# A hybrid decoder trunk on one core: part of the second MLP product by seven block products instead of eight

## The chip, the core and the metric

The kernel runs on one core of one Trainium2 chip. The time is device microseconds of one execution. TensorE (PE) multiplies, VectorE (DVE) and ScalarE (ACT) do everything elementwise, GpSimd (POOL) only builds two small tables at the start, and SyncE (SP) issues the loads of the weights.

## What is computed

Two decoder layers over 256 tokens of width 2048, all in float32. The mixer of a layer (latent attention and retention) is not touched by the change; what follows it is:

```python
h = rmsnorm(x, mlp_norm[l])
x = x + jnp.square(jax.nn.relu(h @ w_up[l])) @ w_down[l]     # w_up 2048 x 8192, w_down 8192 x 2048
...
return rmsnorm(x, final_norm)
```

## The kernel before

**Numbers in two parts.** Each float32 value that PE multiplies is split into a high part, rounded to the multiplier's format, and a low part, the rest. A product is hi·hi + hi·lo + lo·hi. Activations lie with features on partitions and the 256 tokens along the free axis. In `mac_feat` a 128x128 piece of the weight's high part stays in PE while the activation's high and low parts stream past as 512 columns (L213); then the weight's low part, with the high 256 columns (L214). That is one pair of matmuls, 512 and 256 columns. ACT copies the second half of a PSUM bank out and DVE adds the first half (`join`, L231 and L232).

**The weights' way.** SP loads 512 KB of a weight into one of five `raw` buffers. ACT writes the high part into one of six `w` buffers (L179) and DVE the low part (L180, raw minus high). Such a tile of 128x1024 values feeds eight pairs of matmuls. `proj_feat` takes `nt` column tiles of 128 at once, one PSUM bank each, and goes over all k.

**The MLP** of a layer runs in two blocks of FB = 4096 hidden features. For each block, `w_up` in groups of four column tiles (eight w tiles a group, then four joins, relu², and the split of the result into `u` tiles), then `w_down` in groups of 4, 4, 4, 2, 2 column tiles over the block's 32 `u` tiles; each column tile is joined, multiplied by a row of norm factors (L674) and added to x (L675). In a layer's last block the new x is also scaled and split for the next layer (`xs`, L175/L176) and its squares are summed (L256/L257).

**Order.** The program is written in this order, and a scheduler lays out each engine's instructions ahead of time; each engine then goes through its own list in order, waiting on semaphores. At a group's end the four banks are complete; while DVE joins them, PE goes on with w tiles that were split earlier.

Of the kernel before, what the change touches and what calls it, by code (L numbers as in the profile page):

```python
# [11 lines left out]
F32 = mybir.dt.float32  # L12
# [6 lines left out]
P = 128  # L19
# [13 lines left out]

UP_TILES = 4
OUT_GROUPS = [(0, 4), (4, 4), (8, 4), (12, 2), (14, 2)]
END_GROUPS = [(0, 4), (4, 4), (8, 4), (12, 2), (14, 1), (15, 1)]
N_RAW, N_SPLIT = 5, 6

LONGER_ONES, LONGER_XS, LONGER_ROOT = 8, 24, 23

ROUND = 1.5 * 2.0 ** 23

# [43 lines left out]
def kernel(ctx: ExitStack, tc: tile.TileContext, xt, positions, w_in, w_uq, w_ukv, w_o, w_up, w_down,  # L88
# [20 lines left out]
    def w_tile(shape):  # L109
        return wpool.tile(shape, F32R, tag="w", name="w", bufs=N_SPLIT)  # L110

    def w_load(src, shape):
        raw = wpool.tile(shape, F32, tag="raw", name="raw", bufs=N_RAW)
# [23 lines left out]
    def gcol(i):  # L137
        return gain[:, i:i + 1]
# [173 lines left out]

    def norm_tiles():
        acc = cpool.tile([P, T], F32, tag="ssq", name="ssq")
        return acc, []

    def norm_step(acc, tiles, j, g0):
# [5 lines left out]
        tiles.append(xs)  # L323
        if acc is not None:
            add_square(acc, x[j], j == 0)

    acc, xs = norm_tiles()
    for j in range(KD):
        norm_step(None, xs, j, G_ATTN)

    def first_squares():
        for j in range(KD):
# [4 lines left out]
    for l in range(DEPTH):  # L337
        g0 = l * G_LAYER

        with tc.tile_pool(name=f"mix{l}", bufs=1) as ap:  # L340
# [290 lines left out]
            for c0, nt in OUT_GROUPS:  # L631
                for n, ps in enumerate(proj_feat(w_o[l], 0, c0 * P, mixed, nt)):
                    j = c0 + n
                    t = tmp()
                    join(ps, t)
                    nc.vector.tensor_tensor(x[j], x[j], t, op=ALU.add)
                    norm_step(acc, ms, j, g0 + G_MLP)


        with tc.tile_pool(name=f"mlp{l}", bufs=1) as up:  # L640
            rows = {}

            def square_rows(acc=acc):
                yield
                r2 = norm_col([acc], D)
                r22 = col("r22")
                nc.vector.tensor_tensor(r22, r2, r2, op=ALU.mult)
                yield
                yield
# [4 lines left out]
            acc_n, xs_n = norm_tiles() if not last_layer else (cpool.tile([P, T], F32, tag="ssq", name="ssq"), None)  # L654
            for b in range(FF // FB):
                us = []
                for c in range(0, FB, UP_TILES * P):
                    for ps in proj_feat(w_up[l], 0, b * FB + c, ms, UP_TILES):
                        t = tmp()
# [5 lines left out]
                end = last_layer and b == FF // FB - 1  # L665
                if end:
                    root = spool.tile([P, 1 + LONGER_ROOT], F32, tag="root", name="root", bufs=1)[:, 0:1]
                    nc.scalar.sqrt(root, ones)
                for c0, nt in END_GROUPS if end else OUT_GROUPS:
                    for n, ps in enumerate(proj_feat(w_down[l], b * FB, c0 * P, us, nt)):  # L670
                        j = c0 + n
                        t = tmp()
                        join(ps, t)
                        nc.vector.tensor_tensor(t, t, rows["rs2b"], op=ALU.mult)  # L674
                        nc.vector.tensor_tensor(x[j], x[j], t, op=ALU.add)  # L675
                        if end:
                            if j < KD - 1:
                                add_square(acc_n, x[j], j == 0)
                            else:
                                last_sq = tmp("sq", 2)  # L680
                                nc.scalar.activation(last_sq, x[j], AF.Square)
                            nc.scalar.activation(x[j], x[j], AF.Copy, scale=gcol(G_FINAL + j))
                        elif b == FF // FB - 1:
                            norm_step(acc_n, xs_n, j, (l + 1) * G_LAYER + G_ATTN)
            acc, xs = acc_n, xs_n


# [7 lines left out]

    keep_warm(8)
    v = col("nv")
    mean_squares(v, [acc, last_sq], D, EPS)
# [37 lines left out]
```

## Time and profile before

| what | value |
|---|---|
| median of three runs | 2185.0 us (2184.48 to 2185.58) |
| the profiled execution | 2185.49 us, its span 2183.7 us |
| TensorE's mean granted clock | 0.997 |
| busy: PE, PEld (weight loads), DVE, ACT | 99%, 87%, 66%, 49% of the span |
| DMA | 400 MB, mean 183 GB/s |

A busy share is the part of the span in which an engine had an instruction running; the chain of the page follows the work that ended last back to its start, and a wait is time in which an engine stood still, put down to whatever came last.

### The profile page before, as it was taken

How to read it: one execution, taken by the hardware profiler on the slowest of the kernel's cores; microseconds unless marked ns; L12 is line 12 of the kernel's file. 1: busy time of each engine (PE TensorE's matmuls, PEld its weight loads, DVE VectorE, ACT ScalarE, POOL GpSimd, SP SyncE). 2: the span in 40 equal slices, each digit the busy share in tenths (PEclk: the TensorE clock that was granted, in tenths of full speed). 3: DMA queues.
4: the chain of work that ended last, by engine and by line, in shares of the span. 5: the costliest groups of instructions: out<-in, count | busy, mean ns of one | idle time of the engine just before them, and what ended most of it. 6: DMA issues, size and time to landing. Idle time of an engine off the chain costs nothing.

```text
span 2183.7 us, 32563 instructions
## 1 busy us (share of the span) xinstructions
PE 2162.2 (99%) x12566; PEld 1907.8 (87%) x12566; DVE 1433.5 (66%) x2487; ACT 1077.9 (49%) x1658; POOL 24.2 (1%) x34
## 2 busy tenths in 40 slices
PE   7999999999999999999999999999999999999998
PEld 6888888888888888888898888888888888888887
DVE  8878976656555556655668888666665555655554
ACT  7555555545443444444455554555454344544453
POOL 4000000000000000000000000000000000000000
PEclk9999999999999999999999999999999999999999
DMA  7555556666556666555655555566665566665553
GB/s 245 170 160 179 151 188 192 183 194 184 197 180 200 184 194 192 188 190 192 189 173 151 174 164 173 174 198 188 192 189 189 193 187 191 185 196 189 192 183 97
DMA packets 273115, 400.07 MB, mean 183 GB/s; under 512 B 12608, under 2 KB 143808, under 8 KB 272960
## 3 DMA queue, kind: packets, MB, share of 16 engines
q1 hardware_dynamic: 272000, 397.08, 58.7%
q8 instruction: 98, 1.61, 0.3%
q10 hardware_dynamic: 960, 0.92, 0.1%
q14 instruction: 57, 0.47, 0.1%
HBM read 395.85 MB, written 2.10 MB: 182 GB/s over the span
## 4 chain that ended last, share of the span: by engine, by line
PE 98%; DVE 1%; ACT 0%; issue 0%; DMA 0%; SPq 0%; DVEq 0%
PE mm L213 57%; PE mm L214 29%; PE mm L218 3%; PE mm L219 1%; PE at L213 1%; PE at L214 1%; PE at L483 0%; PE at L484 0%; PE mm L368 0%; PE mm L367 0%; PE mm L369 0%; PE at L218 0%; PE at L516 0%; PE at L545 0%; DVE xs L176 0%
## 5 line engine op out<-in xcount | busy, mean ns | idle before, releaser
L180 DVE TENSOR_TENSOR w<-raw,w 128x1024 fp32r<-128x1024 f32 (+3 forms) x792 | 921.9, 1170 | 673.9 <-ACT w L179 673.0
L179 ACT CAST w<-raw 128x1024 fp32r<-128x1024 f32 (+3 forms) x792 | 795.3, 1008 | 887.6 <-PE mm L214 828.3
L213 PE MATMUL mm<-xs,w 128*128 128x512 f32 x2944 | 1032.6, 394 | 8.6 <-ACT w L179 8.6
L214 PE MATMUL mm<-xs,w 128*128 128x256 f32 x2944 | 824.2, 280 | 2.6 <-DVE w L180 2.4
L213 PE MATMUL mm<-u,w 128*128 128x512 f32 x2048 | 710.2, 392 | 0.0
L213 PEld LDWEIGHTS mm<-xs,w 128*128 128x128 f32 x2944 | 553.8, 188 | 129.4 <-ACT w L179 8.9
L214 PE MATMUL mm<-u,w 128*128 128x256 f32 x2048 | 572.4, 280 | 0.0
L214 PEld LDWEIGHTS mm<-xs,w 128*128 128x128 f32 x2944 | 553.9, 188 | 5.1 <-DVE w L180 4.8
L213 PEld LDWEIGHTS mm<-u,w 128*128 128x128 f32 x2048 | 384.4, 188 | 85.1
L214 PEld LDWEIGHTS mm<-u,w 128*128 128x128 f32 x2048 | 384.3, 188 | 0.0
L213 PE MATMUL mm<-mix,w 128*128 128x512 f32 x512 | 177.8, 392 | 0.0
L231 ACT COPY tb<-mm 128x256 f32<-128x256 f32 x280 | 99.6, 372 | 88.5 <-PE mm L214 84.5
L214 PE MATMUL mm<-mix,w 128*128 128x256 f32 x512 | 143.1, 280 | 0.0
L232 DVE TENSOR_TENSOR t<-mm,tb 128x256 f32<-128x256 f32 x280 | 108.2, 418 | 30.7 <-ACT tb L231 30.2
L213 PEld LDWEIGHTS mm<-mix,w 128*128 128x128 f32 x512 | 96.1, 188 | 21.1
L214 PEld LDWEIGHTS mm<-mix,w 128*128 128x128 f32 x512 | 96.1, 188 | 0.0
L218 PE MATMUL mm<-w,xs 128*128 128x512 f32 x256 | 93.0, 401 | 0.0
L219 PE MATMUL mm<-w,xs 128*128 128x256 f32 x256 | 71.7, 280 | 0.0
L172 ACT CAST u<-t 128x256 fp32r<-128x256 f32 x128 | 48.6, 405 | 27.4 <-DVE t L661 27.4
L218 PEld LDWEIGHTS mm<-w,xs 128*128 128x128 f32 x256 | 48.1, 188 | 10.7
L173 DVE TENSOR_TENSOR u<-t,u 128x256 fp32r<-128x256 f32 x128 | 48.9, 422 | 2.8
L219 PEld LDWEIGHTS mm<-w,xs 128*128 128x128 f32 x256 | 48.2, 188 | 0.0
(176 smaller groups left out, 1107.0 us busy)
## 6 DMA issues: line engine op xcount, KB each, us to landing
raw<-w_up SPq DMA_DIRECT2D x256, 512.0 KB, 4.4
raw<-w_down SPq DMA_DIRECT2D x256, 512.0 KB, 3.9
raw<-w_in SPq DMA_DIRECT2D x144, 512.0 KB, 4.6
raw<-w_o SPq DMA_DIRECT2D x64, 512.0 KB, 4.3
raw<-w_uq SPq DMA_DIRECT2D x16, 384.0 KB, 4.2
raw<-w_in SPq DMA_DIRECT2D x16, 320.0 KB, 3.1
raw<-w_ukv SPq DMA_DIRECT2D x8, 512.0 KB, 4.1
x<-xt SPq DMA_DIRECT2D x8, 256.0 KB, 6.7
```

What stands on the lines that cost most here:

```text
L172: nc.scalar.copy(head, src)
L173: nc.vector.tensor_tensor(dst[:, 1, :], src, head.bitcast(F32), op=ALU.subtract)
L179: nc.scalar.copy(dst_h, src)
L180: nc.vector.tensor_tensor(dst_l, src, dst_h.bitcast(F32), op=ALU.subtract)
L213: nc.tensor.matmul(ps, wk[:, 0, n0:n0 + P], act.rearrange("p s t -> p (s t)"), start=first, stop=False)
L214: nc.tensor.matmul(ps[:, 0:T], wk[:, 1, n0:n0 + P], act[:, 0, :], start=False, stop=last)
L218: nc.tensor.matmul(ps, act[:, 0, t0:t0 + P], wk, start=first, stop=False)
L219: nc.tensor.matmul(ps[:, 0:256], act[:, 1, t0:t0 + P], wk[:, 0], start=False, stop=last)
L231: nc.scalar.copy(tb, ps[:, T:2 * T])
L232: nc.vector.tensor_tensor(dst, ps[:, 0:T], tb, op=ALU.add)
```

## The change

Of the 2048 columns of `w_down`, the first 768 (six of the sixteen column tiles) are no longer done tile by tile. For each pair of hidden-feature tiles (u tiles 2k and 2k+1) the tokens are cut into two halves of 128, the hidden features into the two tiles, and the 768 columns into two halves of 384. The product of these 2x2 blocks is made from seven block products (Winograd's form of Strassen's scheme): four sums of `u` blocks (`first_factors`) and four of weight blocks (`second_factors`) are factors beside the plain blocks, and seven PSUM banks collect the products over the block's eight pairs. Here the `u` block stays in PE and 384 weight columns stream past, three matmuls to a product, 21 for a pair. The other ten column tiles are done singly (`next_tile`, in the eighth bank), one after each pair and two at the end; a layer's last block has none after pairs 3 and 7 and four at the end. FB falls from 4096 to 2048, so a layer has four blocks of 16 `u` tiles and not two of 32. At a block's end the seven banks are added to seven sums in SBUF (`gather_products`), at a layer's end the sums are combined, turned by 24 transposes in both layers together, and added to x. The norm factors are multiplied onto `u` (L760) instead of onto the outputs. In the changed file the lines of the helpers lie ten further down: L179/L180 is L189/L190, L213/L214 is L223/L224, L232 is L242, L173 is L183.

```diff
-FB = 4096
+FB = 2048
...
+SB = 384
+SN = 2 * SB // P
+TILE_AFTER, LAST_TILE_AFTER = range(8), (0, 1, 2, 4, 5, 6)
...
+MOVING = 16
...
-    def tmp(tag="t", bufs=4):
+    def tmp(tag="t", bufs=6):
...
+            def first_factors(k, t0, t1):
+
+                f = up.tile([P, 2, 4, P], F32R, tag=f"f{k}", name=f"f{k}")
+                sa, sb = tmp("t"), tmp("t")
+                nc.vector.tensor_tensor(sa[:, 0:P], t0[:, P:T], t1[:, P:T], op=ALU.subtract)
+                nc.vector.tensor_tensor(sa[:, P:T], t0[:, 0:P], t0[:, P:T], op=ALU.subtract)
+                nc.vector.tensor_tensor(sb[:, 0:P], sa[:, 0:P], t0[:, 0:P], op=ALU.subtract)
+                nc.vector.scalar_tensor_tensor(sb[:, P:T], sb[:, 0:P], -1.0, t1[:, 0:P], op0=ALU.mult, op1=ALU.subtract)
+                for i, q in enumerate((sa, sb)):
+                    split(f[:, :, 2 * i:2 * i + 2, :], q.rearrange("p (i t) -> p i t", i=2))
+                return f
+
+            def second_factors(r0):
+
+                raws = [w_load(w_down[l][r0 + k * P:r0 + (k + 1) * P, 0:2 * SB], [P, 1, 2 * SB])[:, 0, :] for k in range(2)]
+                w11, w12, w21, w22 = (r[:, n * SB:(n + 1) * SB] for r in raws for n in range(2))
...
+                parts([w11], w11)
+                parts([w21, w22], raws[1])
+                sums = [wpool.tile([P, 2, SB], F32, tag="raw", name="raw", bufs=N_RAW) for _ in range(2)]
+                nc.vector.tensor_tensor(sums[0][:, 0, :], w11, w12, op=ALU.add)
+                nc.vector.tensor_tensor(sums[0][:, 1, :], w22, w12, op=ALU.add)
+                parts("13", sums[0].rearrange("p i c -> p (i c)"))
+                nc.vector.tensor_tensor(sums[1][:, 0, :], sums[0][:, 0, :], w22, op=ALU.add)
+                nc.vector.tensor_tensor(sums[1][:, 1, :], sums[1][:, 0, :], w21, op=ALU.add)
+                parts("24", sums[1].rearrange("p i c -> p (i c)"))
...
+            def seven_products(ps, us, f, k, r0, first, last):
...
+                for i, a, w in ((1, a11, w11), (2, a12, w21), (3, s4, w22), (5, s1, t1), (7, s3, t3), (6, s2, t2), (4, a22, t4)):
+                    for n, (p, q) in enumerate(((0, 0), (0, 1), (1, 0))):
+                        nc.tensor.matmul(ps[i], a[:, p, :], w[:, q, :], start=first and n == 0, stop=last and n == 2)
+
+            def gather_products(ps, sums, first):
+                for i in (1, 2, 3, 5, 7, 6, 4):
+                    if first:
+                        sums[i] = up.tile([P, SB], F32, tag=f"p{i}", name=f"p{i}")
+                        nc.scalar.copy(sums[i], ps[i])
+                    else:
+                        nc.vector.tensor_tensor(sums[i], sums[i], ps[i], op=ALU.add)
+
+            def join_products(q):
+
+                for o, a, b, op in ((2, 1, 2, ALU.add), (6, 1, 6, ALU.add), (7, 6, 7, ALU.add), (4, 7, 4, ALU.add),
+                                    (7, 7, 5, ALU.subtract), (6, 6, 5, ALU.subtract), (3, 6, 3, ALU.add)):
+                    nc.vector.tensor_tensor(q[o], q[a], q[b], op=op)
+                return (q[2], q[4]), (q[3], q[7])
...
+                        for t in range(2):
+                            nc.tensor.transpose(xT[:, t * P:(t + 1) * P], blocks[n][t][:, f * P:(f + 1) * P], ident)
+                        nc.vector.tensor_tensor(x[j], x[j], xT[:, 0:T], op=ALU.subtract if n else ALU.add)
+                        done_x(j)
...
                         nc.vector.scalar_tensor_tensor(t, t, 0.0, t, op0=ALU.max, op1=ALU.mult)
+                        nc.vector.tensor_tensor(t, t, rows["rs2b"], op=ALU.mult)
...
+                        if before is not None:
+                            fs.append(first_factors(len(fs), before, t))
...
+                for k, f in enumerate(fs):
+                    seven_products(pp, us, f, k, b * FB + 2 * k * P, k == 0, k == len(fs) - 1)
+                    if k in (LAST_TILE_AFTER if end else TILE_AFTER):
+                        next_tile()
+                gather_products(pp, sums, b == 0)
+                if end:
+                    blocks = join_products(sums)
+                    while len(tiles) > 1:
+                        next_tile()
+                    add_blocks(blocks)
+                while tiles:
+                    next_tile()
```

**DVE where `w_up` gives way to `w_down` (layer 0).** Before, DVE's list has the last joins of a group, its relu² (L661) and the low parts of the `u` tiles (L173) beside splits of weights; a row is line, operation, output and inputs, and "x15" repeats it:

```order
L232 TENSOR_TENSOR t<-mm,tb 128x256 x2
L173 TENSOR_TENSOR u_8883<-t,u_8883 128x256
L173 TENSOR_TENSOR u_8891<-t,u_8891 128x256
L661 SCALAR_TENSOR_TENSOR t<-t 128x256 x2
L180 TENSOR_TENSOR w<-raw,w 128x2x512
L173 TENSOR_TENSOR u_8899<-t,u_8899 128x256
L173 TENSOR_TENSOR u_8907<-t,u_8907 128x256
L180 TENSOR_TENSOR w<-raw,w 128x2x512 x15
```

Of the changed kernel this is the same place, from the first join after the last group of `w_up`; `f` is a factor tile, and the weight tile in the middle is the second half of the first single column tile:

```order
L242 TENSOR_TENSOR t<-mm,tb 128x256 x2
L759 SCALAR_TENSOR_TENSOR t<-t 128x256 x2
L760 TENSOR_TENSOR t<-t,rs2b 128x256 x2
L685 TENSOR_TENSOR t<-t 128x128
L684 TENSOR_TENSOR t<-t 128x128
L190 TENSOR_TENSOR w<-raw,w 128x8x128
L183 TENSOR_TENSOR u_5058<-t,u_5058 128x256
L183 TENSOR_TENSOR u_5067<-t,u_5067 128x256
L686 TENSOR_TENSOR t<-t 128x128
L183 TENSOR_TENSOR f_5070<-t,f_5070 128x256
L687 SCALAR_TENSOR_TENSOR t<-t 128x128
L242 TENSOR_TENSOR t<-mm,tb 128x256 x2
```

The same list nine rows further on, to the first weight tile of the second single column tile (the last row holds its two halves):

```order
L183 TENSOR_TENSOR f_5099<-t,f_5099 128x256
L687 SCALAR_TENSOR_TENSOR t<-t 128x128
L190 TENSOR_TENSOR w<-raw,w 128x768
L183 TENSOR_TENSOR f_5099<-t,f_5099 128x256
L708 TENSOR_TENSOR raw<-raw 128x384
L710 TENSOR_TENSOR raw<-raw 128x384
L711 TENSOR_TENSOR raw<-raw 128x384
L190 TENSOR_TENSOR w<-raw,w 128x768
L242 TENSOR_TENSOR t<-mm,tb 128x256
L190 TENSOR_TENSOR w<-raw,w 128x768
L777 TENSOR_TENSOR x_85<-x_85,t 128x256
L190 TENSOR_TENSOR w<-raw,w 128x8x128 x2
```

The nine rows between the two pieces repeat the kinds of the first (a factor's low part, relu², the multiplication, two `u` tiles, two rows of 128 columns) and end with the split of 384 columns and another row of 128. Where fifteen splits of weights followed each other, the group's elementwise work, the factors of two pairs of u tiles and the weights of one whole pair now stand ahead of the second single tile's first split.

**PE at the same place.** Before, the first matmuls on `u` follow the last on `xs` with the same pattern:

```order
L214 MATMUL mm<-xs_4154,w 128x256
L213 MATMUL mm<-xs_4154,w 128x512
L214 MATMUL mm<-xs_4154,w 128x256
L213 MATMUL mm<-u_4367,w 128x512
L214 MATMUL mm<-u_4367,w 128x256
```

In the changed kernel the seven products of pair 0 come first (L724), then tile 0:

```order
L224 MATMUL mm<-xs_4154,w 128x256
L724 MATMUL mm<-w,u_4368 128x384 x3
L724 MATMUL mm<-w,u_4377 128x384 x3
L724 MATMUL mm<-w,f_4380 128x384 x12
L724 MATMUL mm<-w,u_4397 128x384
L724 MATMUL mm<-w,u_4406 128x384
L724 MATMUL mm<-w,f_4409 128x384
L724 MATMUL mm<-w,u_4377 128x384 x3
L223 MATMUL mm<-u_4368,w 128x512
```

The first products of pair 1 (on u_4397, u_4406 and f_4409, high part by high part) now stand ahead of pair 0's last product (u_4377, x3); they need pair 1's weights.

**DVE at the end of a layer.** Before, a column tile's join, multiplication and addition are followed by splits of weights, with x scaled for the next layer between them:

```order
L232 TENSOR_TENSOR t<-mm,tb 128x256 x2
L674 TENSOR_TENSOR t<-t,rs2b 128x256 x2
L675 TENSOR_TENSOR x_97<-x_97,t 128x256 x2
L180 TENSOR_TENSOR w<-raw,w 128x4x256
L176 SCALAR_TENSOR_TENSOR xs_10248<-x_97,gain,xs_10248 128x256
```

In the changed kernel this stands between the join of the sixth single tile, which PE does ahead of pair 7, and the first split of the seventh, which PE does right behind pair 7:

```order
L732 TENSOR_TENSOR p_5847<-p_5847,mm 128x384
L732 TENSOR_TENSOR p_5849<-p_5849,mm 128x384
L186 SCALAR_TENSOR_TENSOR xs_11015<-x_95,gain,xs_11015 128x256
L267 TENSOR_TENSOR ssq<-ssq,sq 128x256
L732 TENSOR_TENSOR p_5851<-p_5851,mm 128x384
L732 TENSOR_TENSOR p_5853<-p_5853,mm 128x384
L732 TENSOR_TENSOR p_5855<-p_5855,mm 128x384
L732 TENSOR_TENSOR p_5857<-p_5857,mm 128x384
L738 TENSOR_TENSOR p_5847<-p_5845,p_5847 128x384
L738 TENSOR_TENSOR p_5855<-p_5845,p_5855 128x384
L190 TENSOR_TENSOR w<-raw,w 128x8x128
```

Ahead of these rows are the join, the sum p_5845 and the addition to x. All seven sums, each of which waits for its product of pair 7, and two of the combinations now precede that split.

## Rows read from the trace of the kernel before

**Rows 1.** The page, busy time by engine, and the chain that ended last.

```profile
PE 2162.2 (99%) x12566; PEld 1907.8 (87%) x12566; DVE 1433.5 (66%) x2487; ACT 1077.9 (49%) x1658; POOL 24.2 (1%) x34
...
PE 98%; DVE 1%; ACT 0%; issue 0%; DMA 0%; SPq 0%; DVEq 0%
```

**Rows 2.** PE's waits, whole run: line waited for, us in total, times, longest.

```profile
PE mm L213 <- ACT w L179: 8.6, 2, 7.7
PE mm L214 <- DVE w L180: 2.4, 3, 0.9
```

**Rows 3.** Windows: length, busy us (instructions) by engine, PE clock, DMA share, GB/s.

```profile
14.00:18.00 4.00, 2.45 (x13) 1.58 (x12) 3.50 (x6) 3.17 (x7) 3.58 (x6) 1.00 1.10 352
18.00:22.00 4.00, 4.00 (x16) 3.31 (x14) 3.90 (x7) 3.05 (x8) 3.58 (x6) 0.57 1.08 343
740.00:910.00 170.00, 170.00 (x983) 149.65 (x982) 103.03 (x146) 82.68 (x118) 0.00 (x0) 1.00 0.63 189
920.00:1085.00 165.00, 165.00 (x954) 145.23 (x954) 96.11 (x129) 78.17 (x102) 0.00 (x0) 1.00 0.58 192
2135.00:2140.00 5.00, 5.00 (x31) 4.42 (x30) 2.08 (x2) 2.11 (x2) 0.00 (x0) 1.00 0.87 240
```

**Rows 4.** PE's timeline, steady stretches: start, duration, line, shape.

```profile
45.75 0.31 PE L367 MATMUL mm<-w,xs 128*128 128x320 f32 x1
...
51.91 0.31 PE L367 MATMUL mm<-w,xs 128*128 128x320 f32 x1
...
899.82 0.39 PE L213 MATMUL mm<-xs,w 128*128 128x512 f32 x1
900.05 0.28 PE L214 MATMUL mm<-xs,w 128*128 128x256 f32 x1
...
911.96 0.39 PE L213 MATMUL mm<-xs,w 128*128 128x512 f32 x1
```

**Rows 5.** PE's timeline at six transposes (L412).

```profile
68.01 0.82 PE L412 MATMUL at<-cst,kv_nat 128*128 128x128 f32 x6
68.58 0.48 PE L213 MATMUL mm<-xs,w 128*128 128x512 f32 x1
```

**Rows 6.** DVE's timeline in the last block: start, duration, in brackets idle before.

```profile
2125.66 0.42 DVE L232 TENSOR_TENSOR t<-mm,tb 128x256 f32<-128x256 f32 x1
...
2127.33 0.42 DVE L232 TENSOR_TENSOR t<-mm,tb 128x256 f32<-128x256 f32 x1
...
2129.46 1.22 DVE L180 TENSOR_TENSOR w<-raw,w 128x1024 fp32r<-128x1024 f32 x1
2130.60 0.42 DVE L675 TENSOR_TENSOR x<-x,t 128x256 f32<-128x256 f32 x1
```

**Rows 7.** Timeline of all engines behind the last column tile.

```profile
2168.25 0.28 PE L214 MATMUL mm<-u,w 128*128 128x256 f32 x1
...
2168.57 0.37 ACT L231 COPY tb<-mm 128x256 f32<-128x256 f32 x1 [8.35 <-PE mm L214]
2168.97 0.42 DVE L232 TENSOR_TENSOR t<-mm,tb 128x256 f32<-128x256 f32 x1 [8.84 <-ACT tb L231]
2169.43 0.42 DVE L674 TENSOR_TENSOR t<-t,rs2b 128x256 f32<-128x256 f32 x1
```

**Rows 8.** Timeline of DVE and PE where `w_up` gives way to `w_down`.

```profile
914.43 0.75 DVE L232 TENSOR_TENSOR t<-mm,tb 128x256 f32<-128x256 f32 x2
...
914.73 0.39 PE L213 MATMUL mm<-u,w 128*128 128x512 f32 x1
```

**Rows 9.** Groups of instructions by form: count, busy us and mean ns, idle before.

```profile
L179 ACT CAST w<-raw 128x1024 fp32r<-128x1024 f32 x728 | 766.7, 1054 | 865.9 <-PE mm L214 807.1 <-PE mm L219 27.7 <-issue 19.6
L179 ACT CAST w<-raw 128x640 fp32r<-128x640 f32 x16 | 11.4, 724 | 6.6 <-PE mm L214 6.1 <-PE mm L369 0.4
...
L180 DVE TENSOR_TENSOR w<-raw,w 128x1024 fp32r<-128x1024 f32 x728 | 890.2, 1226 | 666.6 <-ACT w L179 665.8
```

**Rows 10.** The page, DMA issues: count, KB each, median us to landing.

```profile
raw<-w_down SPq DMA_DIRECT2D x256, 512.0 KB, 3.9
```

More of the change, by code (lines that the diff above doesn't have):

```diff
@@ L103, in abank, with w_tile @@
         return pspool.tile([P, 512], F32, tag="ps", name="at")
-    def tmp(tag="t", bufs=4):
+    def tmp(tag="t", bufs=6):
         return tpool.tile([P, T], F32, tag=tag, name=tag, bufs=bufs)
-    def w_tile(shape):
-        return wpool.tile(shape, F32R, tag="w", name="w", bufs=N_SPLIT)
+    def w_tile(shape, moving=False):
+        n = math.prod(shape[1:])
+        o = MOVING if moving else 0
+        t = wpool.tile([P, max(n, 2048) + 2 * MOVING], F32R, tag="w", name="w", bufs=N_SPLIT)[:, o:o + n]
+        names = "abc"[:len(shape) - 1]
+        return t.rearrange(f"p ({' '.join(names)}) -> p {' '.join(names)}", **dict(zip(names, shape[1:])))
     def w_load(src, shape):
@@ L314, in norm_tiles, with norm_tile @@
         acc = cpool.tile([P, T], F32, tag="ssq", name="ssq")
-        return acc, []
-    def norm_step(acc, tiles, j, g0):
+        return acc, [None] * KD
+    def norm_tile(j, g0):
         more = LONGER_XS if j == KD - 1 else 0
@@ L322, in norm_step @@
         split(xs, x[j], gcol(g0 + j))
-        tiles.append(xs)
-        if acc is not None:
-            add_square(acc, x[j], j == 0)
+        return xs
     acc, xs = norm_tiles()
     for j in range(KD):
-        norm_step(None, xs, j, G_ATTN)
+        xs[j] = norm_tile(j, G_ATTN)
     def first_squares():
@@ L654, with done_x @@
             acc_n, xs_n = norm_tiles() if not last_layer else (cpool.tile([P, T], F32, tag="ssq", name="ssq"), None)
+            squared = []
+            def done_x(j):
+                if not last_layer:
+                    xs_n[j] = norm_tile(j, (l + 1) * G_LAYER + G_ATTN)
+                    add_square(acc_n, x[j], not squared)
+                elif len(squared) < KD - 1:
+                    add_square(acc_n, x[j], not squared)
+                else:
+                    last_squares.append(tmp("sq", 2))
+                    nc.scalar.activation(last_squares[0], x[j], AF.Square)
+                squared.append(j)
+                if last_layer:
+                    nc.scalar.activation(x[j], x[j], AF.Copy, scale=gcol(G_FINAL + j))
@@ new lines, in second_factors, with parts @@
+            def second_factors(r0):
+                raws = [w_load(w_down[l][r0 + k * P:r0 + (k + 1) * P, 0:2 * SB], [P, 1, 2 * SB])[:, 0, :] for k in range(2)]
+                w11, w12, w21, w22 = (r[:, n * SB:(n + 1) * SB] for r in raws for n in range(2))
+                out = []
+                def parts(srcs, src):
+                    n = len(srcs) * SB
+                    ws = w_tile([P, 2, n], True)
+                    split_w(ws[:, 0, :], ws[:, 1, :], src)
+                    out.extend(ws[:, :, i * SB:(i + 1) * SB] for i in range(len(srcs)))
+                parts([w11], w11)
[7 more added lines that the diff above has]
+                parts("24", sums[1].rearrange("p i c -> p (i c)"))
+                weave()
+                return out
@@ new lines, in add_blocks @@
+            def add_blocks(blocks):
+                for n in range(2):
+                    for f in range(SB // P):
+                        j = n * (SB // P) + f
+                        xT = abank()
+                        for t in range(2):
+                            nc.tensor.transpose(xT[:, t * P:(t + 1) * P], blocks[n][t][:, f * P:(f + 1) * P], ident)
+                        nc.vector.tensor_tensor(x[j], x[j], xT[:, 0:T], op=ALU.subtract if n else ALU.add)
+                        done_x(j)
@@ L655 @@
+            last_squares, sums = [], {}
             for b in range(FF // FB):
-                us = []
+                us, fs, end = [], [], b == FF // FB - 1
+                before = None
                 for c in range(0, FB, UP_TILES * P):
                     for ps in proj_feat(w_up[l], 0, b * FB + c, ms, UP_TILES):
-                        t = tmp()
+                        t = tmp("t", 6)
                         join(ps, t)
                         nc.vector.scalar_tensor_tensor(t, t, 0.0, t, op0=ALU.max, op1=ALU.mult)
+                        nc.vector.tensor_tensor(t, t, rows["rs2b"], op=ALU.mult)
@@ L664 @@
                         us.append(u)
-                end = last_layer and b == FF // FB - 1
-                if end:
+                        if before is not None:
+                            fs.append(first_factors(len(fs), before, t))
+                        before = t if before is None else None
+                if end and last_layer:
                     root = spool.tile([P, 1 + LONGER_ROOT], F32, tag="root", name="root", bufs=1)[:, 0:1]
                     nc.scalar.sqrt(root, ones)
[L669 to L684, printed above, removed]
@@ new lines, with next_tile @@
+                tiles = deque(range(SN, KD))
+                def next_tile():
+                    j = tiles.popleft()
+                    ps, = proj_feat(w_down[l], b * FB, j * P, us, 1)
+                    t = tmp("t", 6)
+                    join(ps, t)
+                    nc.vector.tensor_tensor(x[j], x[j], t, op=ALU.add)
+                    if end:
+                        done_x(j)
+                pp = {i: bank()[:, 0:SB] for i in (1, 2, 3, 5, 7, 6, 4)}
+                for k, f in enumerate(fs):
+                    seven_products(pp, us, f, k, b * FB + 2 * k * P, k == 0, k == len(fs) - 1)
+                    if k in (LAST_TILE_AFTER if end else TILE_AFTER):
+                        next_tile()
@@ L685 @@
+                gather_products(pp, sums, b == 0)
+                if end:
+                    blocks = join_products(sums)
[4 more added lines that the diff above has]
+                    next_tile()
             acc, xs = acc_n, xs_n
```

12 lines of the change are left out of this document (8 added, 4 removed).

## The prediction

> **What bounds the kernel now.** I read the page first, then PE's waits, then windows inside the MLP, then single rows. On the page PE is busy 99% of the span and the chain that ended last is PE for 98% [rows 1]: DVE at 66% and ACT at 49% are covered. PE's waits for split weights come to 11.0 us in the whole run, 7.7 of it in one wait [rows 2]. In a stretch of `w_up` PE is busy for 170.00 of 170 us with DVE at 103.03 (61%), in one of `w_down` for 165.00 of 165 with DVE at 96.11 (58%) [rows 3]. So a matmul less is time saved, as long as the split weights come in time. The profiled execution took 2185.49 us, 0.5 above the median of 2185.0; my sum is made against it. About 0.2%, 4.4 us, is what a measurement of this kernel can tell from no change.
>
> **What PE saves.** 35 pairs of 512 and 256 columns start from 899.82 to 911.96, 0.3469 us a pair; 42 matmuls of 320 columns from 45.75 to 51.91, 0.1467 each [rows 4]. A time per column and one per matmul that fit both are 0.419 ns and 0.0127 us, which makes 384 columns 0.1735 us. (Between bounds: 0.1734 is half the pair of 768 columns, 0.1760 the rate of the 320.) A pair of u tiles times 768 columns was 12 pairs of matmuls, 4.163 us, and is now 21 x 0.1735 = 3.643: 0.520 less. There are 8 blocks of 8 pairs, so 64 x 0.520 = 33.3 us less (29.9 with 0.1760). Added are 24 transposes; six took from 68.01 to 68.58, 0.095 each [rows 5], so 2.3 us. Off the tail comes one dependent DVE step, 2168.97 to 2169.43 [rows 7], 0.46 us. PE's sum alone is -31.5 us.
>
> **What DVE must now do, and where it is late.** Prices: back to back, five instructions of 256 columns start 1.67 us apart, 0.333 each, and one of 1024 takes 1.14 to the next start [rows 6]; a straight line through these gives 0.20 for 128 columns, 0.467 for 384, 0.87 for 768. The work is added in four places.
>
> (1) *From w_up to w_down, eight times (four of them are new, since the blocks are halved).* Before, PE had up to six w tiles of eight matmul pairs, 6 x 2.78 = 16.7 us of work, to run on while DVE joined. Now the tiles split ahead are pair 0's four (3.64 us of PE, for the same six slots) and tile 0's two (5.55). DVE's list after the group's end, up to the second tile's first split, holds 22 instructions of 256 columns (joins, relu², the new multiplication, low parts of u and f, one x), 8 of 128, 4 of 384, 3 of 768 and 2 of 1024: 22 x 0.333 + 8 x 0.20 + 4 x 0.467 + 3 x 0.87 + 1.14, and 1.22 for the last one's duration, make 15.8 us. It starts 0.30 before PE's first matmul behind the group [rows 8], so that split is done 15.5 us after the group's end. PE wants it after pair 0, tile 0, pair 1 and the 0.23 us of the first 512-column matmul [rows 4]: 3.64 + 5.55 + 3.64 + 0.23 = 13.06. Late by 2.4 us, eight times 19.3 us. In the trace it should show in pieces: in pair 0 ahead of its last product, since three products of pair 1, whose 768 columns ACT casts late, stand ahead of it; in pair 1 before the fourth product; and at tile 1. Bounds: had each instruction no fixed part, the 39 would be some 2.5 us shorter and nothing late; if each of the 22 waited for its predecessor at the 0.46 of [rows 7], 2.8 longer, 5.2 late, 42 us in all. I take the first figure: nearly every one has an unrelated instruction between it and what it needs.
>
> [...] By full durations the list would be about 3 us longer and the eight places would cost some 45 us; the measured spacing decides.
>
> (2) *The steady cycle of one pair and one tile, 9.2 us of PE.* When a tile ends, ACT copies its second half out, then casts a pair of weight sums (768 columns, about 0.83 between 0.724 for 640 and 1.054 for 1024 [rows 9]), then casts the next tile; DVE's low part follows: 0.37 + 0.83 + 1.05 + 1.23 and hand-offs of 0.03 to 0.04 [rows 7] make 3.6 us. PE wants it after one pair and a 512-column matmul: 3.87. So it is hidden by 0.26 us. DVE's total of 7.9 us in 9.2 fits. Cost 0; if the cover is gone, 0.2 us in each of some 45 cycles.
>
> (3) *Gathers in the other six blocks.* In a layer's second and third block two sums of 384 stand ahead of the last woven tile's split: 0.44 (PE's end to DVE, [rows 7]) + 0.333 + 0.467 + 0.333 + 0.87 + 0.467 + 1.22 = 4.13 against 3.87. In the first block ACT copies the seven banks instead, beside the same casts. I take 0.26 for each of six, 1.6 us.
>
> (4) *The two layer ends.* Pair 7 covers 3.87 us, but seven sums, two combinations, join, addition and, in layer 0, x's scaling and squares stand ahead of the next split: 0.44 + 0.333 + 0.467 + 0.333 + 0.93 + 0.67 + 1.87 + 0.93 + 1.22 = 7.2, late by 3.3; in layer 1 a split of 768 stands there in place of the scaling, late by 3.8. With that scaling and squares on ACT ahead of three tiles in layer 0 (0.5 to 0.65 each) and a little in layer 1: 9.3 us.
>
> The multiplication by norm factors moves from x's path to u's; it is counted in (1). DMA: single tiles come in 512 B runs, as in the window 2135:2140, which ran at 0.87 of the queues for a tile every 2.8 us without a stall [rows 3]; the new cycle loads two such tiles and two of 384 KB in 9.2 us, about two thirds, and w_down lands 3.9 us after issue [rows 10], which the buffers cover except just behind place (1).
>
> **Sum.** -31.5 + 19.3 + 1.6 + 9.3 = -1.3. To this I add the clock: after PE had stood for some 1.5 us of 14:18, the granted clock of 18:22 was 0.57, between its levels of 1.2 and 2.4 GHz, and 16 matmuls ran where the steady stretch has 23 [rows 3], so about 1.2 us lost. Ten stalls of two to four microseconds come here, mostly in pieces; I take two such falls, 2.5 us. That gives 2185.5 + 1.2, about 2187 us.
>
> **Rivals.** *PE stays the bound and the stalls are hidden.* For it: 39 to 42% of DVE is idle in the MLP [rows 3], and a scheduler may have placed work where PE's lead is larger than I count. Against it: the order of DVE's list at the group's end. With no stall 2154, with half 2169. A rule gives the same outcome: the Trainium skill's "Perfetto Trace Analysis", section "Identifying the Most-Contended Engine", says to improve the engine of highest occupancy first, which before is PE in every window; it does not say what a slower helper takes back.
>
> *The clock falls at every transition.* The places are the ten of (1) and (4); if each costs 1.2 us, as at 18:22, the time is 2185.5 - 1.3 + 12 = 2196. It decides against the change once each stall is long enough to lower the clock; against it, the mean granted clock of the whole run is 0.997 in spite of its waits.
>
> *DVE is dearer than back to back.* In place (1) the dependent price, or 0.2 us more in a steady cycle: 10 to 20 us more, 2197 to 2207. It decides as soon as a cycle overruns its 0.26 us. For it: ACT and DVE hand over four times in each cycle, and I have counted each hand-off at its shortest.
>
> *The 384-column matmul runs at 0.1760*: 3.4 us more than forecast, inside its range.
>
> **How the numbers follow.** The forecast, most of the saving eaten by stalls, has 0.45 and spans 2178 to 2196 (1 us either way at each of eight transitions); of it 0.05 lies below 2181.1, 0.28 within 0.2%, 0.12 above 2189.9. Hidden stalls: 0.24, faster. The clock: 0.13, slower. Dear DVE: 0.18, slower. Together 0.29 faster, 0.28 within 0.2%, 0.43 slower. The range of 2169 to 2205 leaves out the half of the first rival with less than half of the stalls (0.12) and the end of the last (0.05).
>
> **What would show it.** Right: L724 starts 0.173 us apart; PE waits for ACT and DVE (L189, L190) of 2 to 3 us in sum behind each of eight groups of `w_up`, 3 to 4 at each layer's end, next to none in the cycles between; PE's busy share 97 to 98%; DVE up to about 75%. Wrong: no waits behind the groups (then the first rival), waits in every cycle (the third), a granted clock under 1 behind each transition (the second), or L724 spaced wider than 0.176.

## The result and the profile after

The changed kernel takes 2210.4 us, median of four runs (2209.5 to 2211.1), against 2185.0 for the one before: a ratio of 1.0116, 95% interval 1.0099 to 1.0134. It is slower by 25 us. The forecast of 2187 and its range up to 2205 were too low.

The profiled execution spans 2208.6 us, before 2183.7. Its page gives busy time by engine and the chain that ended last, beside [rows 1]:

```profile
PE 2159.2 (98%) x12398; PEld 1910.3 (86%) x12398; DVE 1794.2 (81%) x3451; ACT 1219.0 (55%) x1976; POOL 24.5 (1%) x34
...
PE 78%; DVE 12%; DMA 6%; ACT 2%; issue 1%; SPq 0%; ACTq 0%; DVEq 0%
```

PE was 98% of the chain; now DVE holds 12% and DMA 6%. PE's busy 98% hides this, since a matmul that was held up is itself drawn longer (0.44 us at 474.96 below, where its neighbours have 0.34). PE's waits in the whole run (line waited for, us in total, times, longest), beside [rows 2]:

```profile
PE mm L223 <- ACT w L189: 13.4, 5, 7.3
PE mm L224 <- DVE w L190: 12.5, 23, 2.5
PE mm L724 <- DVE t L242: 7.6, 8, 1.0
PE mm L724 <- ACT w L189: 3.9, 12, 1.2
PE mm L724 <- DVE w L190: 0.9, 4, 0.4
```

38 us. Of these 12.6 stand in the first 36 us, ahead of the MLP, where the kernel before had its 11.0, so some 26 are left for the MLP. For the rest one has to lay PE's start times against its steady pace. I use 0.3469 us for a 512/256 pair [rows 4] and 0.1735 for 384 columns; a pair of u tiles is then 3.64, a column tile 5.55.

**One of the eight transitions**, PE's timeline (start, duration, line, shape, count, idle before):

```profile
471.31 1.21 PE L724 MATMUL mm<-w,u 128*128 128x384 f32 x6
472.36 2.24 PE L724 MATMUL mm<-w,f 128*128 128x384 f32 x12
474.44 0.34 PE L724 MATMUL mm<-w,u 128*128 128x384 f32 x1
...
474.96 0.44 PE L724 MATMUL mm<-w,u 128*128 128x384 f32 x1 [0.18 <-ACT w L189]
...
476.52 0.76 PE L724 MATMUL mm<-w,u 128*128 128x384 f32 x3 [0.95 <-DVE t L242]
...
487.01 0.39 PE L224 MATMUL mm<-u,w 128*128 128x256 f32 x1 [0.28 <-DVE w L190]
...
492.44 1.21 PE L724 MATMUL mm<-w,u 128*128 128x384 f32 x6
```

Twelve matmuls run from 472.36 to 474.44, 0.173 each. From 471.31, the group's end, to 492.44, pair 2's start, pass 21.13 us for 18.38 of work: 2.75 late. Seven of the eight places lose 2.75 within 0.02, the last 2.92: 22.2 in all. DVE's list there, beside [rows 8]:

```profile
471.00 0.75 DVE L242 TENSOR_TENSOR t<-mm,tb 128x256 f32<-128x256 f32 x2
...
475.96 0.74 DVE L242 TENSOR_TENSOR t<-mm,tb 128x256 f32<-128x256 f32 x2
...
485.74 1.21 DVE L190 TENSOR_TENSOR w<-raw,w 128x1024 fp32r<-128x1024 f32 x1
```

It ends at 486.95, 15.6 us behind the group, with no idle time marked in it. The join at 475.96 is the third of the four waiting: it frees the PSUM bank that pair 0's last product needs.

**The cycles behind it.** In the six blocks that don't end a layer, from pair 2's start to the next `w_up` there is 66.26 us of work, and it took 68.64, 68.01, 67.48, 68.53, 67.64 and 68.61: 11.4 us, in pieces of 0.1 to 0.7. Of these 3.4 stand at the last woven tile, beside the gather, 0.5 to 0.7 in each block; 8.0 are left for the cycles. ACT's and DVE's rows of one cycle:

```profile
495.71 1.05 ACT L189 CAST w<-raw 128x1024 fp32r<-128x1024 f32 x1 [0.57 <-DMA raw<-w_down]
...
496.79 1.22 DVE L190 TENSOR_TENSOR w<-raw,w 128x1024 fp32r<-128x1024 f32 x1 [0.39 <-ACT w L189]
...
498.33 0.51 ACT L189 CAST w<-raw 128x384 fp32r<-128x384 f32 x1 [1.57 <-DMA raw<-w_down]
```

Here ACT waits for a load, then DVE for ACT. PE feels it in the next pair, 0.35 late at 505.02. The rows that lead there, in order of time (SPq is the queue that issues loads):

```profile
491.85 0.95 DVE L190 TENSOR_TENSOR w<-raw,w 128x768 fp32r<-128x768 f32 x1
492.83 0.34 SPq L124 DMA_DIRECT2D raw<-w_down  x1
...
498.88 0.56 DVE L190 TENSOR_TENSOR w<-raw,w 128x384 fp32r<-128x384 f32 x1 [0.86 <-ACT w L189]
...
502.50 0.55 DVE L711 TENSOR_TENSOR raw<-raw 128x384 f32<-128x384 f32 x1
503.14 2.73 ACT L189 CAST w<-raw 128x768 fp32r<-128x768 f32 x3 [0.68 <-DVE raw L711]
...
505.02 0.62 PE L724 MATMUL mm<-w,f 128*128 128x384 f32 x2 [0.19 <-DVE w L190]
```

Read backwards: PE waits for the low part of the pair's last two sums (DVE, 504.01), this for ACT's cast of them (503.14), this for the fourth sum (502.50). Ahead of the sum DVE has no idle time back to 498.88, the low part of the columns that ACT cast at 498.33. The load which that cast waited for landed at 498.23. It was issued at 492.83, when DVE's split of the first two sums of the pair before (491.85 to 492.80) had freed its buffer. Five more stalls of 0.2 to 0.6 in the cycles go back to a load in the same way. Over the run, ACT's wait of that kind:

```profile
ACT w L189 <- DMA raw<-w_down: 124.8, 142, 2.8
```

**The layer ends.** Pairs 2 to 7, eight tiles and the transposes are 67.46 us of work. They took 78.30 in layer 0 (1026.41 to 1104.71) and 77.60 in layer 1: 10.8 and 10.1 lost, 21.0 together. PE's timeline in layer 0, pair 3 first and then the stretch behind pair 7:

```profile
1036.43 1.21 PE L724 MATMUL mm<-w,u 128*128 128x384 f32 x6
...
1043.22 0.62 PE L724 MATMUL mm<-w,f 128*128 128x384 f32 x2 [1.18 <-ACT w L189]
1044.29 1.15 PE L724 MATMUL mm<-w,f 128*128 128x384 f32 x5 [0.44 <-ACT w L189]
...
1046.14 0.40 PE L223 MATMUL mm<-u,w 128*128 128x512 f32 x1
...
1075.07 0.40 PE L223 MATMUL mm<-u,w 128*128 128x512 f32 x1
1078.63 0.50 PE L223 MATMUL mm<-u,w 128*128 128x512 f32 x1 [3.17 <-ACT w L189]
1080.13 0.58 PE L224 MATMUL mm<-u,w 128*128 128x256 f32 x1 [1.00 <-DVE w L190]
1080.51 0.63 PE L223 MATMUL mm<-u,w 128*128 128x512 f32 x1
...
1081.15 0.63 PE L223 MATMUL mm<-u,w 128*128 128x512 f32 x1
...
1083.49 0.39 PE L223 MATMUL mm<-u,w 128*128 128x512 f32 x1
```

Pairs 3 and 4 stand back to back, since `LAST_TILE_AFTER` has no 3, and take 9.71 us for 7.3 (1036.43 to 1046.14). Behind pair 7 PE waits 3.17 and 1.00, and from 1080.51 pairs start 0.64 us apart and not 0.347. Two windows (length, busy us and instructions by engine, clock, DMA share, GB/s) show the clock there and at a transition, beside [rows 3]:

```profile
470.00:478.00 8.00, 6.87 (x38) 6.01 (x37) 8.00 (x22) 4.84 (x11) 0.00 (x0) 1.00 0.22 64
1075.00:1085.00 10.00, 5.83 (x24) 4.55 (x23) 10.00 (x18) 5.34 (x7) 0.00 (x0) 0.83 0.86 219
```

The clock falls behind the long wait, where it costs some 1.3 us (four pairs, 0.3 each), and not behind the 1.1 us of pieces at 470. DVE's rows ahead of that wait:

```profile
1071.34 2.02 DVE L190 TENSOR_TENSOR w<-raw,w 128x768 fp32r<-128x768 f32 x2
1073.27 0.42 DVE L242 TENSOR_TENSOR t<-mm,tb 128x256 f32<-128x256 f32 x1
...
1077.92 1.02 DVE L738 TENSOR_TENSOR p<-p,p 128x384 f32<-128x384 f32 x2
1078.86 1.22 DVE L190 TENSOR_TENSOR w<-raw,w 128x1024 fp32r<-128x1024 f32 x1
```

The join at 1073.27 belongs to a tile that PE ended at 1071.41. Pair 7's last weights stand ahead of it, themselves late.

**The account.** 33.3 saved, less 2.4 for transposes (1.2 a layer), is 30.9; stalls of 22.2 + 11.4 + 21.0 are 54.6. That is +23.7 of the 24.9 us between the spans; about 1 us is not placed.

### The profile page after: what moved, and what is told of

Its sections match the earlier page's. It is cut to its first block, busy times and chain, and to the rows that moved or that the text cites. A ratio compares the mean times of both kernels' runs of the same rounds, so it can differ in the third digit from the quotient of the medians.

```text
span 2208.6 us, 33675 instructions
## 1 busy us (share of the span) xinstructions
PE 2159.2 (98%) x12398; PEld 1910.3 (86%) x12398; DVE 1794.2 (81%) x3451; ACT 1219.0 (55%) x1976; POOL 24.5 (1%) x34
## 4 chain that ended last, share of the span: by engine, by line
PE 78%; DVE 12%; DMA 6%; ACT 2%; issue 1%; SPq 0%; ACTq 0%; DVEq 0%
PE mm L223 42%; PE mm L224 22%; DMA raw<-w_down 6%; DVE w L190 5%; PE mm L228 3%; PE mm L724 3%; ACT w L189 2%; PE mm L229 1%; PE at L223 1%; DVE raw L708 1%; PE at L224 1%; DVE t L242 1%; DVE raw L710 1%; DVE raw L707 1%; PE at L492 0%
## 5 line engine op out<-in xcount | busy, mean ns | idle before, releaser
L190 DVE TENSOR_TENSOR w<-raw,w 128x1024 fp32r<-128x1024 f32 (+5 forms) x952 | 1014.9, 1077 | 324.9 <-ACT w L189 320.0
L189 ACT CAST w<-raw 128x1024 fp32r<-128x1024 f32 (+5 forms) x952 | 877.7, 933 | 666.7 <-PE mm L224 420.2
L223 PE MATMUL mm<-xs,w 128*128 128x512 f32 x2944 | 1032.6, 394 | 7.7 <-ACT w L189 7.7
L224 PE MATMUL mm<-xs,w 128*128 128x256 f32 x2944 | 826.9, 281 | 4.9 <-DVE w L190 4.9
L223 PEld LDWEIGHTS mm<-xs,w 128*128 128x128 f32 x2944 | 553.2, 188 | 126.4 <-ACT w L189 8.0
L224 PEld LDWEIGHTS mm<-xs,w 128*128 128x128 f32 x2944 | 555.1, 189 | 7.4 <-DVE w L190 7.1
L223 PE MATMUL mm<-u,w 128*128 128x512 f32 x1280 | 452.5, 393 | 5.8 <-ACT w L189 5.8
L224 PE MATMUL mm<-u,w 128*128 128x256 f32 x1280 | 365.5, 286 | 7.7 <-DVE w L190 7.6
L223 PEld LDWEIGHTS mm<-u,w 128*128 128x128 f32 x1280 | 241.7, 189 | 54.8 <-ACT w L189 6.9
L224 PEld LDWEIGHTS mm<-u,w 128*128 128x128 f32 x1280 | 242.5, 189 | 21.5 <-DVE w L190 21.0
L223 PE MATMUL mm<-mix,w 128*128 128x512 f32 x512 | 178.0, 391 | 0.0
L724 PE MATMUL mm<-w,f 128*128 128x384 f32 x768 | 155.3, 342 | 4.4 <-ACT w L189 2.5
L724 PEld LDWEIGHTS mm<-w,f 128*128 128x128 f32 x768 | 132.1, 188 | 15.6 <-DVE w L190 7.3
L224 PE MATMUL mm<-mix,w 128*128 128x256 f32 x512 | 143.7, 281 | 0.0
L242 DVE TENSOR_TENSOR t<-mm,tb 128x256 f32<-128x256 f32 x296 | 116.9, 417 | 29.9 <-ACT tb L241 28.9
L724 PE MATMUL mm<-w,u 128*128 128x384 f32 x576 | 127.7, 340 | 9.1 <-DVE t L242 7.6
L223 PEld LDWEIGHTS mm<-mix,w 128*128 128x128 f32 x512 | 96.1, 188 | 20.8
L724 PEld LDWEIGHTS mm<-w,u 128*128 128x128 f32 x576 | 98.8, 188 | 17.1 <-issue 9.9
L182 ACT CAST f<-t 128x256 fp32r<-128x256 f32 x128 | 52.1, 407 | 83.3 <-DVE t L687 44.4
L224 PEld LDWEIGHTS mm<-mix,w 128*128 128x128 f32 x512 | 96.4, 188 | 0.0
```

What stands on the lines that cost most here:

```text
L189: nc.scalar.copy(dst_h, src)
L190: nc.vector.tensor_tensor(dst_l, src, dst_h.bitcast(F32), op=ALU.subtract)
L223: nc.tensor.matmul(ps, wk[:, 0, n0:n0 + P], act.rearrange("p s t -> p (s t)"), start=first, stop=False)
L224: nc.tensor.matmul(ps[:, 0:T], wk[:, 1, n0:n0 + P], act[:, 0, :], start=False, stop=last)
L724: nc.tensor.matmul(ps[i], a[:, p, :], w[:, q, :], start=first and n == 0, stop=last and n == 2)
```

## The experiments

Each is an edit of the changed kernel unless it says otherwise. Each has one run beside a run of the kernel before on the same chip (2185.3 to 2185.6), and where an interval is given, four against seven.

**1. A single tile behind every pair of the last block.**
```
-TILE_AFTER, LAST_TILE_AFTER = range(8), (0, 1, 2, 4, 5, 6)
+TILE_AFTER, LAST_TILE_AFTER = range(8), range(7)
```


> A layer's last block weaves a single tile after each of pairs 0 to 6, so after pair 3 too (three tiles are left for the end, not four). Theory A, DVE's list sets the end: pairs 3 and 4 back to back need 9.9 us of DVE in 7.3 us of PE and lost 2.4 us in each layer, with 0.8 more around them; with a tile between that is gone and the end of the layer stays: 2204 to 2206 us. Rival, PE itself (its clock or the 384-column matmuls) is slow: the same number of matmuls, no change, 2210.

2207.97 us, 2.5 less, where 4 to 6 were expected. The stall in pairs 3 and 4 of layer 0 is gone (tiles there lose 0.3), but with a tile fewer left behind pair 7, 6.9 us are lost there. The place was rightly named, and part of its time moved on.

**2. The four sums of weights on GpSimd.**
```
-nc.vector.tensor_tensor(sums[0][:, 0, :], w11, w12, op=ALU.add)
+nc.gpsimd.tensor_tensor(sums[0][:, 0, :], w11, w12, op=ALU.add)
...
```


> The four weight sums of a pair (384 columns each) go from DVE to GpSimd, nothing else changes. Theory A: DVE has 1.9 us less in each pair, so the waits after a group fall from 2.7 to about 1 us (14 us in all), the small waits of the cycles (12 us) nearly vanish and pairs 3 and 4 of the last block keep pace (5 us): 2180 to 2190. Rival: GpSimd takes over 1 us for a sum, four in a chain take longer than DVE did, and the split waits for them: 2210 to 2240. Rival, PE itself: no change.

2271.46, 61 us more, also more than the rival had. The costliest of its four groups of sums, and DVE's splits of 384 columns in this run and then in the changed kernel (count, busy us and mean ns, idle before):

```profile
L711 POOL TENSOR_TENSOR raw<-raw 128x384 f32<-128x384 f32 x64 | 99.5, 1555 | 5.0
...
L190 DVE TENSOR_TENSOR w<-raw,w 128x384 fp32r<-128x384 f32 x64 | 70.8, 1106 | 6.0 <-ACT w L189 6.0
...
L190 DVE TENSOR_TENSOR w<-raw,w 128x384 fp32r<-128x384 f32 x64 | 35.5, 555 | 23.6 <-ACT w L189 23.2
```

1555 ns where DVE takes 550; the four come to 5.8 us a cycle, one behind the other. Nor is DVE spared anything: beside the busy GpSimd its splits of 384 and 768 columns take 1106 and 1280 ns, not 555 and 953, and it is busy for 1829 us in all, with 256 instructions fewer than the 1794 us of the changed kernel. So sums that come later and a slower DVE can each stand behind the loss; this run does not part them.

**3. A single tile ahead of the gather at a layer's end.**
```
+if end:
+    next_tile()
 gather_products(pp, sums, b == 0)
```


> In a layer's last block one single tile is put ahead of gathering the seven sums. Theory A: the stall of 5 us behind pair 7 in each layer (with the slower matmuls after it 6) shrinks to under 2, as that tile's splits no longer stand behind seven sums and two combinations: 2201 to 2204. Rival: the tile takes the eighth bank later than the sums free theirs, and the stall moves behind that tile: 2208 to 2212.

2205.6, 4.8 less. Behind pair 7 of layer 0 about 1.0 is left of 6.1, but PE now waits for the combined sums at the transposes:

```profile
PE at L747 <- DVE p L738: 2.9, 1, 2.9
```

So layer 0's end gains nothing by PE's start times (11.6 lost, 10.8 without the edit), and what is gained is layer 1's (5.6 lost, 10.1 without).

**4. The last group of `w_up` in two halves**, so that half of its elementwise work runs under PE's second half.
```
-UP_TILES = 4
+UP_GROUPS = [(0, 4), (4, 4), (8, 4), (12, 2), (14, 2)]
```


> The last four column tiles of w_up in each block are done as two and two, so two u tiles and one pair of factors are left after the last group, not four and two; PE's work is the same. Theory A: DVE's list behind the group is 11 instructions of 256 and 4 of 128 columns shorter, 4.5 us, and the 2.7 us of waits in each of eight places vanish: 2188 to 2192. Rival: the waits come from ACT's casts and the loads, not DVE's list: 2205 to 2210.

2187.84, 22.6 less. By PE's start times the transitions now lose 2.8 us in all (22.2 before the edit), the cycles 9.2 (11.4), the layer ends 20.3 (21.0). The same window as above:

```profile
470.00:478.00 8.00, 8.00 (x48) 7.47 (x47) 7.77 (x19) 4.39 (x9) 0.00 (x0) 1.00 0.50 156
```

PE is busy throughout, and pair 0 to tile 1 take 3.66, 5.55, 3.65 and 5.60 us; the last block of layer 0 still waits 0.8 and 0.5. The layer ends stay. It is the elementwise work behind the group, set against PE's lead, that made those stalls. The Trainium skill's "Perfetto Trace Analysis", section "Optimizing Scalar/DVE Operations", says that where Scalar or Vector are not saturated but cause bubbles elsewhere, smaller instructions may let work end sooner; that DVE stood at 81% agrees, though here it was the group that was cut, and no instruction.

**5. The kernel before, with blocks of 2048.**
```
-FB = 4096
+FB = 2048
```


> The kernel before with FB = 2048 and nothing else: four blocks a layer, the same matmuls, twice the multiplications and additions to x on DVE. Theory A (what counts is how much elementwise work stands behind a group against the split work ahead of PE): the lead of up to six tiles of 2.8 us covers every new transition, 2185 to 2187. Rival, halving alone makes waits: more than 2190.

2185.67 beside 2185.3: nothing. A transition alone costs nothing where PE's lead is six tiles; in the changed kernel the factors, sums and pair weights behind it, and the shorter lead, do.

**6. Edits 4 and 3 together.**

> Both the last group of w_up in two and two and, at a layer's end, one tile ahead of the gathering. Theory A: the two act at different places, so their gains add up: 2187.8 less 4.8, 2182 to 2184. Rival, they take the same work off: 2186 to 2188.

2186.03, only 1.8 better than edit 4, where 4.8 would have made it 2183.0. By PE's start times the layer ends do gain as under edit 3: they lose 16.7 where edit 4 alone left 20.3 (edit 3 alone took them from 21.0 to 17.2), though in layer 0 pairs 3 and 4 now lose 4.0 and the transposes wait 2.3. What is missing lies in the cycles, which lose 12.2 where edit 4 alone left 9.2. Why is not shown; with one run of each, part of it may be scatter.

**7. Strassen's sums in three blocks of a layer, the last by the old loop**, with edit 4.
```
+if end:
+    for c0, nt in END_GROUPS if last_layer else OUT_GROUPS:
+        for n, ps in enumerate(proj_feat(w_down[l], b * FB, c0 * P, us, nt)):
+            ...
+    continue
...
+if b == FF // FB - 2:
+    add_blocks(join_products(sums))
```


> The block sums in three of a layer's four blocks; the last block does all sixteen column tiles in the groups of before, and the sums are combined, turned and added to x behind the third block, under the last block's w_up. The last group of w_up is halved as well. It loses 16 of 64 pairs' saving (8.3 us) and no longer has the end blocks' waits (10 to 11 us a layer beside the transition). Theory A: 2187.8 + 8.3 - 21, 2172 to 2178. Rival, the waits at the layer's end move with the combinations to the next place: 2185 or more.

2176.07; ratio to before 0.9958, interval 0.9941 to 0.9975: faster than before. It gives back a quarter of the saving (8.3 us) to be rid of the layer ends: the last block's `w_down` runs 88.8 us without a wait, and the sums are combined where nobody waits for them.

**8. The same, with the weight sums in buffers of their own**, not in those that loads land in. Loads get four in place of five, and a tile of split weights is cut to what it uses, for room.
```
-N_RAW, N_SPLIT = 5, 6
+N_RAW, N_SPLIT = 4, 6
-t = wpool.tile([P, max(n, 2048) + 2 * MOVING], ...)
+t = wpool.tile([P, max(n + o, 2048)], ...)
-sums = [wpool.tile([P, 2, SB], F32, tag="raw", name="raw", bufs=N_RAW) for _ in range(2)]
+sums = [wpool.tile([P, 2, SB], F32, tag="wsum", name="wsum", bufs=2) for _ in range(2)]
```


> As three_blocks_of_four, with the weight sums in two buffers of their own and four raw buffers for loads, where both shared five. Theory: the small waits in the cycles, 1 to 2 us in each of six blocks, come from raw weights that land late because sums hold their buffers; then 4 to 8 us less than three_blocks_of_four. Rival, ACT and DVE are late by their own order: no change, or a little more for the fewer load buffers in the plain stages.

2172.77 (2171.9 to 2178.6), ratio 0.9949, interval 0.9934 to 0.9963: the fastest median of all. It is 3.3 below edit 7's, less than the 4 to 8 expected, and one of its four runs lies above all four of edit 7's. ACT's wait for loads falls from 99.4 us there to 32.7, but the cycles and last tiles of the six blocks lose 8.7 us in both profiles, so what the loads' buffers are worth here is not shown. Its main waits (line numbers are one higher):

```profile
PE mm L224 <- ACT w L190: 8.0, 2, 7.5
PE mm L224 <- DVE t L243: 5.4, 8, 1.5
```

The first holds the one that before had (7.7); the second is new, a tile waiting for the join of the single tile before it. In DVE's list that join stands behind a weight sum that itself waits for a load: at 530.62 one lands, the sums start at 530.64 and 531.11, the join at 531.58, and PE goes on at 532.05, 1.7 late.

**9. Edit 7 without the halved group.**

> The changed kernel with only a layer's last block done by the groups of before (sums joined behind the third block), the last group of w_up left at four column tiles. If the end blocks' waits (10.8 and 10.2 us beside the transition) are a part of their own: 2210.4 + 8.3 for the 16 pairs - 21, and one transition a layer fewer into block sums (5.5 together, as the plain groups have a longer lead): 2192 to 2199. Rival, the waits at the layer's end exist only because the transitions leave DVE late: the end gives less than 8 back and the loss of 8.3 eats it, 2208 or more.

2190.57, 19.9 less than the changed kernel and just under what was expected. With the 8.3 given back this puts 28.2 us on the two last blocks, where I count 21.0 and two transitions (5.7), 26.7. The transitions left are 2.75 as before.

**10. The changed kernel with the buffers of edit 8 alone.**

> The changed kernel with only the weight sums in two buffers of their own and four raw buffers. The cycles' small waits were 12 us in sum; if they come from raw weights that land late because sums hold the shared buffers, most goes: 2198 to 2203, with the waits behind the groups and at the layers' ends as they were. Rival, ACT's and DVE's order makes them: 2208 to 2212.

2186.77, 23.7 less, far more than I expected. It is a single run, and the kernels with these buffers scatter more than the others (edits 8, 11 and 12 over 7 to 9 us, edit 7 and the changed kernel over 1 to 2), so the size is sure to some microseconds only. ACT's wait for loads, the window at the layer's end and the one at the first transition:

```profile
ACT w L189 <- DMA raw<-w_down: 42.6, 66, 1.9
```
```profile
1075.00:1085.00 10.00, 9.04 (x53) 7.93 (x53) 9.41 (x15) 3.46 (x7) 0.00 (x0) 1.00 0.61 165
470.00:478.00 8.00, 6.68 (x34) 5.58 (x33) 8.00 (x22) 5.61 (x13) 0.00 (x0) 0.93 0.44 129
```

By PE's start times the transitions lose 20.0 (22.2), the cycles and last tiles 3.3 (11.4), the layer ends 8.1 (21.0). The clock no longer falls at 1075 to 1085, but it does at three transitions and in pair 4 of layer 0's last block. In this run, then, most of the cycles' loss and more than half of the ends' is gone with the sums out of the loads' buffers. But ACT's wait has partly changed its name: for the sums of L708 and L711 it now waits 119.2 us, not 54.7. The scheduler's order changed as well: splits of pair 7's sums and one of a tile's now stand earlier in DVE's list, and three transitions, those where the clock falls, lose about 4 us, the others 1.3 to 2.1. How much the buffers did and how much the order, this run does not part, and edits 8 and 11, with the same buffers, lose in the cycles as much as without them or more.

**11. Edits 4 and 10 together.**

> The changed kernel, block sums in all four blocks, with both the last group of w_up in two and two and the sums in their own buffers. Theory, two causes at different places: own buffers alone left 2 to 4 us behind each group of w_up, which the halved group takes away: 2186.8 less 16 to 22, 2165 to 2171, under the 2172.8 of three blocks. Rival, both give DVE the same slack: 2182 to 2187.

2175.46 (2171.4 to 2180.2), ratio 0.9954, interval 0.9935 to 0.9972. The two do not add (2164 would be the sum): the transitions are gone, but the cycles and last tiles lose 14.1, where edit 10 alone left 3.3. PE waits 8.3 us for joins (L223 <- DVE t L242), and these stand in DVE's list behind sums that wait for a load, as in edit 8.

**12. Edits 1, 4 and 10 together.**

> As halved_and_own_buffers, with a single tile after each of pairs 0 to 6 of a layer's last block too. Theory A: pairs 3 and 4 back to back still lose about 3.5 us in each layer there, which the tile between them saves: 4 to 7 us under halved_and_own_buffers. Rival, the shorter end (three tiles) loses it again: within 2 us of it.

2175.17 (2171.7 to 2180.4), ratio 0.9955, interval 0.9939 to 0.997: no different from the one before, as the rival had it. A wait of 4.0 us now stands in the next layer's first product.

## Why the prediction was wrong

**PE's saving** was right: 0.1733 measured for the 384-column matmul, 0.1735 forecast. The rival of 0.1760 falls.

**Step (1), the transitions**, was right in mechanism, place and nearly in size: DVE's list of 39 instructions ended 15.6 us behind the group (15.5 forecast), the stall came in the pieces named, and was 2.75 us (2.4), together 22.2 (19.3). Halving the group took nearly all of that away. By full durations, which the prediction weighed, the list would have been longer: they add up to 18.9 us, and it took 15.95 from first start to last end.

**Step (2), nothing in the cycles, and (3), 1.6 us for gathers**, came to 8.0 and 3.4. Step (3) was right in place and too small (0.5 to 0.7 a block, 0.26 forecast). Step (2) was wrong. DVE's work in a cycle was priced well (7.95 us busy in the one from 1610.17 to 1619.39, 7.9 forecast), though its share of the whole span is 81%, where I had "up to about 75%". What failed is the sentence on loads, "which the buffers cover except just behind place (1)". I counted bytes and the time from issue to landing, not how long a buffer is held. Two of five raw buffers hold sums until ACT and DVE have split them, so loads are issued late, as the one at 492.83 was. They also land later: the page has a median of 4.9 us for the new loads of 384 KB, and I had reckoned with 3.9. ACT waits 124.8 us for loads, and a margin of 0.26 us had to bear it.

That late loads make the stalls in the cycles is shown for the six longest, which were followed back; the others, of 0.1 to 0.3 us, were not. How much of it the sums in the loads' buffers did is open. Buffers of their own left 3.3 us of the loss in edit 10, but 8.7 in edit 8 and 14.1 in edit 11, where PE's stalls still go back to a load, now over a join. The Trainium skill's "Perfetto Trace Analysis", section "Optimization Strategy", says that the same gap repeating on the engine that should be saturated can mean too few buffers for the next tile. The trace agrees as far as the load at 492.83 goes, which waited 1.8 us, from the issue before it, for a buffer to come free.

**Step (4), the layer ends at 9.3**, was 21.0, or 18.4 without the clock, which I had priced apart. Three things were missing. Pairs 3 and 4 stand without a tile between them (2.4 in layer 0, 2.5 in layer 1; the change's own tuple says so, and edit 1 took it away). DVE began the list that I had priced at 7.2 us with the join 1.86 us behind the tile's end, where I had allowed 0.44, because pair 7's weights were late. And the other places from pair 2 to pair 7 lose some 2 us in each layer (at most 0.8 a tile), where I had 2.2 for both together.

**The clock** was sized rightly (two falls, 2.5; measured 2 x 1.3) but belongs to the two ends alone. The rival in which it falls at each transition is refuted for this kernel: 1.00 at 470 to 478. In edit 10, though, it fell at three of the eight.

**The rivals.** Hidden stalls: no. Dear DVE, at 2197 to 2207, came nearest, as the one that has each cycle overrun its margin; but in the cycles the cause was late loads, not the price of an instruction. The range's upper end rested on one such mishap alone, while three terms were off together: 2.9 for (1), 9.8 for (2) and (3) and 9.1 for (4) make 21.8 of the 23.4 us by which the time missed the forecast.

**Where the saving went.** Off PE's path as planned, 31 us; given back as stalls of the engines that feed it, 55. With the transitions and either the buffers or the layer ends mended it shows at last, 9 to 12.5 us of it (edits 7, 8, 11). Stalls mended at one place came back in part at another (edits 1, 3, 6, 11, 12). DVE stays busy for 81 to 83% of the span in these, which may be why; no run shows it.

## What to carry to other kernels

When work moves from the bound engine to its helpers, price the places where PE's lead is short, and then ask of each new tile whose buffer it takes and until when: a sum kept in a load's buffer can delay a transfer that byte counts show as covered. Read a schedule's exceptions (a tuple that skips an index, an end handled apart) as places of their own. If a block's end costs more than its share of the saving, do that block the old way.

## What the runs showed of the hardware

GpSimd took 1297 to 1555 ns for an addition of 128 x 384 fp32 beside a busy DVE, which does it in 550, and DVE slowed down beside it: a split of 384 columns took 1106 ns, 555 without. On the clock, waits of 0.18 and 0.95 us at a transition left it at 1.00 (470 to 478 in the changed kernel), while in edit 10 waits of 0.98 and 0.22 us at the same place took it to 0.93 over 8 us, and 3.17 and 1.00 us close together to 0.83 over 10 us. Behind both falls the pairs of matmuls start 0.64 us apart and not 0.347: that is the lower of its two levels, 1.2 GHz. So short waits can cost the clock too, and the longest wait alone does not tell whether they will.
